# Layernorm with residual: x and residual loaded 16 rows at a time instead of 8, the stores moved ahead of the residual loads, and the last residual load split in 120 and 8 partitions

## The chip, the cores and the metric

The kernel runs on one core of a Trainium2 chip. The metric is device time in microseconds (us). The profiled span is about 1.3 us shorter than the time of the same execution. A transfer "lands" when the last increment of its semaphore comes; the trace of the kernel before shows 16 increments for each load of x or residual and each store, and does not name the DMA engines that they come from. The DMA share is the page's: the mean busy share of the core's 16 DMA engines.

In this text ACT is ScalarE, DVE is VectorE, POOL is GpSimd and SP is SyncE, which issues the loads of x and residual and all stores. "Row" is one row of 512 float32 (2 KB) in each of the 128 partitions; the problem has 128 such rows, and 8 of them are 2 MB.

## The reference

```python
def reference(x, residual, gamma, beta, eps):      # x, residual: [16, 1024, 512] float32
    z = x + residual
    mean = np.mean(z, axis=-1, keepdims=True)
    var = np.var(z, axis=-1, keepdims=True)
    return gamma * (z - mean) / np.sqrt(var + eps) + beta
```

So 67.1 MB are read and 33.6 MB written.

## The kernel before

Each engine has one part of the work. SP loads x into a ring of 64 rows and the residual into a ring of 32 rows, and stores the result out of the x ring. POOL adds 8 rows at a time. ACT takes 4 rows at a time: a pass for the mean, a pass for the sum of squares, and a small square root. DVE follows with two passes for each row, in place.

SP's loop decides the order of the transfers. All go through one queue: the page of the kernel before has 6336 of its 6341 packets in q1, and its 44 transfers landed in the order of their issue, each with its first increment after the last one of the transfer before. So an entry stands behind all that were issued before it:

```python
X_CHUNKS = [8] * 15 + [4, 4]
R_CHUNKS = [8] * 15 + [4, 4]
OUT_CHUNKS = [16] * 7 + [8, 4, 4]
Z_ROWS, R_ROWS, STORE_LAG = 64, 32, 40

    for c, (lo, n) in enumerate(loads_x):
        asked = lo + n
        while stored < asked - Z_ROWS:          # the x ring: wait until a block has been stored
            ...
            nc.sync.wait_ge(so[o], 16)
        move(part(zbuf, Z_ROWS, lo, n), dram(xf, lo, n), sx[c])
        while todo_r and ... <= asked:
            wait_rows(s_add, "add", rlo + rn - R_ROWS)      # the residual ring
            move(part(rbuf, R_ROWS, rlo, rn), dram(rf, rlo, rn), sr[rc])
        while todo_o and (... <= asked - STORE_LAG or asked == total):
            wait_rows(s_out, "out", olo + on)
            move(dram(of, olo, on), part(zbuf, Z_ROWS, olo, on), so[oc])
    ...
    for c, (lo, n) in enumerate(loads_x):       # POOL
        nc.gpsimd.wait_ge(sx[c], 16)
        for rc, (rlo, rn) in enumerate(loads_r):
            if lo <= rlo < lo + n:
                nc.gpsimd.wait_ge(sr[rc], 16)
                for a in range(rlo, rlo + rn, ADD):         # ADD = 8
                    nc.gpsimd.tensor_tensor(out=z, in0=z, in1=..., op=ALU.add).then_inc(s_add, an)
    # ... cut: ACT and DVE loops, 4 rows a group, two groups a turn
```

Of the kernel before, what the change touches and what calls it, by code (L numbers as in the profile page):

```python
# [10 lines left out]
ALU = mybir.AluOpType  # L11


X_CHUNKS = [8] * 15 + [4, 4]
R_CHUNKS = [8] * 15 + [4, 4]
OUT_CHUNKS = [16] * 7 + [8, 4, 4]

Z_ROWS = 64
R_ROWS = 32
STORE_LAG = 40  # L20


ADD = 8
# [11 lines left out]
def kernel(  # L35
# [9 lines left out]
    nc = tc.nc  # L45
    P = nc.NUM_PARTITIONS
    xf = x.flatten_outer_dims()
    rf = residual.flatten_outer_dims()
    of = out.flatten_outer_dims()
    N, D = xf.shape  # L50
    inv_d = 1.0 / float(D)
    total = N // P
# [5 lines left out]
    def spans(sizes):  # L58
        assert sum(sizes) == total
        return [(sum(sizes[:c]), n) for c, n in enumerate(sizes)]  # L60

    blocks = spans(OUT_CHUNKS)

    def dram(t, lo, n):

        b0, bn = next(b for b in blocks if b[0] <= lo and lo + n <= b[0] + b[1])
        v = t[P * b0 : P * (b0 + bn), :].rearrange("(p j) d -> p j d", p=P)
        return v[:, lo - b0 : lo - b0 + n, :].rearrange("p a b -> p (a b)")

    zbuf = nc.alloc_sbuf_tensor("zbuf", [P, Z_ROWS * D], FP32)  # L70
    rbuf = nc.alloc_sbuf_tensor("rbuf", [P, R_ROWS * D], FP32)
# [17 lines left out]
    def sem(name):  # L89
        s = nc.alloc_semaphore(name)  # L90
        sems.append(s)
        return s

    loads_x, loads_r, stores = spans(X_CHUNKS), spans(R_CHUNKS), blocks
    sx = [sem(f"sx{c}") for c in range(len(loads_x))]
    sr = [sem(f"sr{c}") for c in range(len(loads_r))]
# [7 lines left out]
    s_out = sem("out")  # L104
    so = [sem(f"so{c}") for c in range(len(stores))]
# [3 lines left out]
    def part(buf, size, lo, n):  # L109
        assert lo % size + n <= size  # L110
        return buf[:, (lo % size) * D : (lo % size + n) * D]
# [16 lines left out]
    todo_r, todo_o = list(enumerate(loads_r)), list(enumerate(stores))  # L128
# [3 lines left out]
    def wait_rows(s, key, rows):  # L132
        if rows > seen[key]:
            nc.sync.wait_ge(s, rows)
            seen[key] = rows

    def move(out, in_, s):
        i = nc.sync.dma_start(out=out, in_=in_).then_inc(s, 16)  # L138
        if len(first) < EARLY:
            first.append(i.ins)  # L140

    stored = 0
    for c, (lo, n) in enumerate(loads_x):
        asked = lo + n
        while stored < asked - Z_ROWS:
            o = next(i for i, b in enumerate(stores) if b[0] == stored)
            assert all(o != t[0] for t in todo_o)
            nc.sync.wait_ge(so[o], 16)
            stored += stores[o][1]
        move(part(zbuf, Z_ROWS, lo, n), dram(xf, lo, n), sx[c])  # L150
        while todo_r and todo_r[0][1][0] + todo_r[0][1][1] <= asked:
            rc, (rlo, rn) = todo_r.pop(0)
            wait_rows(s_add, "add", rlo + rn - R_ROWS)
            move(part(rbuf, R_ROWS, rlo, rn), dram(rf, rlo, rn), sr[rc])
        while todo_o and (
            todo_o[0][1][0] + todo_o[0][1][1] <= asked - STORE_LAG or asked == total
        ):
            oc, (olo, on) = todo_o.pop(0)
            wait_rows(s_out, "out", olo + on)
            move(dram(of, olo, on), part(zbuf, Z_ROWS, olo, on), so[oc])  # L160



    for o, (lo, n) in enumerate(stores[:-1]):
# [7 lines left out]
    for c, (lo, n) in enumerate(loads_x):  # L172
        nc.gpsimd.wait_ge(sx[c], 16)
        for rc, (rlo, rn) in enumerate(loads_r):
            if lo <= rlo < lo + n:
                assert rlo + rn <= lo + n
                nc.gpsimd.wait_ge(sr[rc], 16)
                for a in range(rlo, rlo + rn, ADD):
                    an = min(ADD, rlo + rn - a)
                    z = part(zbuf, Z_ROWS, a, an)  # L180
                    nc.gpsimd.tensor_tensor(  # L181
                        out=z, in0=z, in1=part(rbuf, R_ROWS, a, an), op=ALU.add
                    ).then_inc(s_add, an)
# [8 lines left out]
    with act.Fori(0, total // LAP) as lap:  # L192
        z0 = act.snap((lap * (LAP * D)) % (Z_ROWS * D))
        r0 = act.snap(lap * LAP)
        for j in range(SETS):
# [4 lines left out]
            for k in range(TURN):  # L200
                i = act.activation(  # L201
                    out=junk_m[k][:, :],
# [7 lines left out]
            for k in range(TURN):  # L210
                i = act.activation(  # L211
                    out=junk_s[k][:, :],
# [8 lines left out]
                out=std[j][:, :],  # L221
# [9 lines left out]
    with dve.Fori(0, total // LAP) as lap:  # L231
        z0 = dve.snap((lap * (LAP * D)) % (Z_ROWS * D))
        r0 = dve.snap(lap * LAP)
        for j in range(SETS):
# [3 lines left out]
            for k in range(TURN):  # L238
                dve.scalar_tensor_tensor(  # L239
                    out=zk[k],  # L240
# [9 lines left out]
            for k in range(TURN):  # L250
                i = dve.scalar_tensor_tensor(  # L251
                    out=zk[k],
# [53 lines left out]
```

## Time and profile before

| | before |
|---|---|
| time, median | 239.19 us (239.16 to 239.43, 4 runs) |
| profiled span | 237.9 us |
| ACT, DVE, POOL busy | 78%, 74%, 60% |
| DMA | 100.7 MB, mean 423 GB/s |

From the page of the kernel before, part 2, the span in 40 equal slices (5.9 us each); a digit is the busy share in tenths, and the last line is what the DMA engines moved:

```profile
ACT  2003999999999999999999999739996399999600
POOL 0098988989889407893078930889209892770000
DMA  8999999999999999999999999999999999999996
GB/s 309 441 433 421 433 433 433 419 427 441 421 438 419 438 427 424 468 441 386 427 433 435 441 413 433 430 449 430 413 430 419 457 441 383 455 435 430 421 417 287
```

DMA is at 9 from the second slice to the next to last. ACT has holes, in the second half too: there it waits for rows. The view by windows of the kernel before puts numbers to it. The columns are the stretch, its length, the busy time (and instructions) of PE, PEld, DVE, ACT and POOL, the clock, the DMA share and GB/s:

```profile
12.00:60.00 48.00, 0.00 (x0) 0.00 (x0) 30.77 (x51) 37.21 (x111) 43.84 (x5) 1.00 1.01 430
...
110.00:169.00 59.00, 0.00 (x0) 0.00 (x0) 49.08 (x81) 51.39 (x152) 35.46 (x4) 1.00 1.00 429
169.00:210.00 41.00, 0.00 (x0) 0.00 (x0) 32.88 (x55) 34.22 (x103) 23.75 (x4) 1.00 1.01 431
210.00:238.00 28.00, 0.00 (x0) 0.00 (x0) 17.92 (x30) 13.22 (x39) 3.02 (x1) 1.00 0.92 396
```

From 110 to 169 us, ACT is busy for 51.39 of 59 us, from 169 to 210 for 34.22 of 41, and DVE for less, while the DMA share is 1.00 and 1.01. The kernel is DMA-bound. The waits view of the kernel before says what ACT's holes wait for (total, times, longest):

```profile
ACT junk_m L201 <- POOL zbuf L181: 29.1, 4, 17.4
```

POOL in turn waits for residual loads, as POOL's timeline of the kernel before shows (start, duration, idle before, releaser). The lines are the adds of rows 96 to 103, 104 to 111 and 112 to 119:

```profile
159.40 8.84 POOL L181 TENSOR_TENSOR zbuf<-zbuf,rbuf 128x4096 f32<-128x4096 f32 x1 [0.90 <-DMA rbuf<-in_residual_dram]
179.00 8.86 POOL L181 TENSOR_TENSOR zbuf<-zbuf,rbuf 128x4096 f32<-128x4096 f32 x1 [10.75 <-DMA rbuf<-in_residual_dram]
188.77 8.85 POOL L181 TENSOR_TENSOR zbuf<-zbuf,rbuf 128x4096 f32<-128x4096 f32 x1 [0.91 <-DMA rbuf<-in_residual_dram]
```

The end of the kernel before, from its timeline: the last two stores are issued, the last ACT group ends with its square root, and DVE ends the last rows:

```profile
223.31 6.12 SPq L138 DMA_DIRECT2D out_dram<-zbuf  x2
223.46 0.30 ACT L220 ACTIVATE std<-ssq,eps_t 128x4 f32<-128x4 f32 x1
...
226.35 2.72 DVE L251 SCALAR_TENSOR_TENSOR zbuf<-zbuf,rstd,beta_p 128x512 f32 x4
```

The last result is ready at 229.1 us, but its store, only 1 MB, lands at 237.86 us (the trace's semaphore increments). The store before it landed at 235.35.

### The profile page before, as it was taken

The numbers are of one execution on the slowest core, as the hardware profiler recorded it, in microseconds if no ns is written. First come the engines' busy times: TensorE is split into PE (matmuls) and PEld (weight loads), VectorE is DVE, ScalarE is ACT, GpSimd is POOL, SyncE is SP. The second block draws the span as 40 slices with busy tenths as digits, with TensorE's granted clock in tenths as the row PEclk, the third lists the DMA queues.
The fourth block names the chain that finished last, engine by engine and source line by source line (L and its number), as shares of the span: only waits on it lengthen the run. The fifth ranks groups of instructions, "written<-read, shape, count | busy, mean of one in ns | idle before, by whom it ended". The sixth has DMA issues, their size and how long they took to land.

```text
span 237.9 us, 1484 instructions
## 1 busy us (share of the span) xinstructions
PE 3.7 (2%) x4; PEld 1.2 (0%) x4; DVE 177.2 (74%) x290; ACT 185.5 (78%) x545; POOL 142.2 (60%) x21
## 2 busy tenths in 40 slices
PE   0600000000000000000000000000000000000000
PEld 0100000000000000000000000000000000000000
DVE  0000498989898989898989898963989549898950
ACT  2003999999999999999999999739996399999600
POOL 0098988989889407893078930889209892770000
DMA  8999999999999999999999999999999999999996
GB/s 309 441 433 421 433 433 433 419 427 441 421 438 419 438 427 424 468 441 386 427 433 435 441 413 433 430 449 430 413 430 419 457 441 383 455 435 430 421 417 287
DMA packets 6341, 100.68 MB, mean 423 GB/s; under 512 B 706, under 2 KB 706, under 8 KB 708
## 3 DMA queue, kind: packets, MB, share of 16 engines
q1 hardware_dynamic: 6336, 100.67, 99.3%
q14 instruction: 1, 0.01, 0.0%
q10 hardware_dynamic: 4, 0.00, 0.0%
HBM read 67.11 MB, written 33.55 MB: 423 GB/s over the span
## 4 chain that ended last, share of the span: by engine, by line
DMA 49%; ACT 24%; POOL 11%; DVE 5%; issue 4%; SPq 1%; ACTq 1%; DVEq 0%; POOLq 0%
DMA rbuf<-in_residual_dram 36%; ACT junk_s L211 14%; DMA out_dram<-zbuf 13%; POOL zbuf L181 11%; ACT junk_m L201 10%; DVE zbuf L239 3%; DVE zbuf L251 3%; SPq L138 1%; ACTq L201 1%; DVEq L239 0%; ACT std L220 0%; DVE rstd L248 0%; ACTq L192 0%; ACTq L198 0%; DVEq L231 0%
## 5 line engine op out<-in xcount | busy, mean ns | idle before, releaser
L181 POOL TENSOR_TENSOR zbuf<-zbuf,rbuf 128x4096 f32<-128x4096 f32 (+1 forms) x17 | 142.0, 8353 | 70.6 <-DMA rbuf<-in_residual_dram 70.6
L239 DVE SCALAR_TENSOR_TENSOR zbuf<-zbuf,nm,gamma_p 128x512 f32 x128 | 87.1, 742 | 48.7 <-ACT junk_s L211 48.7
L201 ACT ACTIVATE junk_m<-zbuf 128x512 f32 x128 | 74.8, 585 | 31.5 <-POOL zbuf L181 29.1
L211 ACT ACTIVATE junk_s<-zbuf,nm 128x512 f32 x128 | 88.9, 695 | 1.0
L251 DVE SCALAR_TENSOR_TENSOR zbuf<-zbuf,rstd,beta_p 128x512 f32 x128 | 87.1, 743 | 1.1
L211 ACT ACTIVATION_READ_ACCUMULATOR junk_s<-zbuf,nm 128x1 f32 x128 | 23.9, 187 | 0.0
L201 ACT ACTIVATION_READ_ACCUMULATOR junk_m<-zbuf 128x1 f32 x128 | 23.9, 186 | 0.0
L220 ACT ACTIVATE std<-ssq,eps_t 128x4 f32<-128x4 f32 x32 | 9.5, 297 | 3.0
L248 DVE RECIPROCAL rstd<-std 128x4 f32<-128x4 f32 x32 | 5.4, 170 | 0.0
L189 ACT ACT_TABLE_LOAD x1 | 1.3, 1283 | 2.7 <-PEq L56 2.7
L123 PE MATMUL gamma_p<-gb_row,ones 1*128 1x512 f32 x2 | 2.0, 1118 | 7.2 <-DMA gb_row<-in_gamma_dram 7.2
L123 PE MATMUL beta_p<-gb_row,ones 1*128 1x512 f32 x2 | 1.9, 1052 | 0.0
L118 DVE MEMSET ones<- 1x128 f32 x1 | 0.2, 165 | 2.0 <-PEq L56 2.0
L123 PEld LDWEIGHTS beta_p<-gb_row,ones 1*128 1x128 f32 x2 | 0.7, 328 | 1.0 <-issue 0.5
L123 PEld LDWEIGHTS gamma_p<-gb_row,ones 1*128 1x128 f32 x2 | 0.5, 308 | 7.2 <-issue 7.2
L287 POOL MEMSET const-float32-0.0<- 128x1 f32 x1 | 0.1, 99 | 0.2 <-issue 0.2
L287 POOL MEMSET const-bfloat16-1.0<- 128x1 bf16 x1 | 0.1, 102 | 0.0
L287 POOL MEMSET const-uint8-127<- 128x1 uint8 x1 | 0.1, 102 | 0.0
L287 POOL MEMSET const-float32-1.0<- 128x1 f32 x1 | 0.1, 99 | 0.0
L119 DVE MEMSET eps_t<- 128x1 f32 x1 | 0.1, 59 | 0.0
## 6 DMA issues: line engine op xcount, KB each, us to landing
zbuf<-in_x_dram SPq DMA_DIRECT2D x15, 2048.0 KB, 32.9
rbuf<-in_residual_dram SPq DMA_DIRECT2D x15, 2048.0 KB, 30.1
out_dram<-zbuf SPq DMA_DIRECT2D x7, 4096.0 KB, 28.5
zbuf<-in_x_dram SPq DMA_DIRECT2D x2, 1024.0 KB, 32.5
rbuf<-in_residual_dram SPq DMA_DIRECT2D x2, 1024.0 KB, 34.5
out_dram<-zbuf SPq DMA_DIRECT2D x1, 2048.0 KB, 15.7
out_dram<-zbuf SPq DMA_DIRECT2D x2, 1024.0 KB, 10.4
gb_row<-in_gamma_dram ACTq DMA_DIRECT2D x1, 2.0 KB
```

Of the source, the lines that this page charges most:

```text
L118: nc.vector.memset(ones[:, :], 1.0).then_inc(s_const, 1)
L123: nc.tensor.matmul(dest[:, :], ones[:, :], gb_row[:, k * D : (k + 1) * D], start=True, stop=True).then_inc(s_pe, 1)
L138: i = nc.sync.dma_start(out=out, in_=in_).then_inc(s, 16)
L181: nc.gpsimd.tensor_tensor(out=z, in0=z, in1=part(rbuf, R_ROWS, a, an), op=ALU.add).then_inc(s_add, an)
L189: act.preload_act_table_set("sqrt_and_others")
L201: i = act.activation(out=junk_m[k][:, :], in_=zk[k], func=ACT.Identity, scale=-inv_d, accum_out=nm[j][:, k : k + 1],)
L211: i = act.activation(out=junk_s[k][:, :], in_=zk[k], func=ACT.Square, bias=nm[j][:, k : k + 1], accum_out=ssq[j][:, k : k + 1],)
L220: act.activation(out=std[j][:, :], in_=ssq[j][:, :], func=ACT.Sqrt, bias=eps_t[:, 0:1], scale=inv_d,).then_inc(s_std, TURN)
L239: dve.scalar_tensor_tensor(out=zk[k], in0=zk[k], scalar=nm[j][:, k : k + 1], in1=gamma_p[:, :], op0=ALU.add, op1=ALU.mult,)
L248: dve.reciprocal(out=rstd[j][:, :], in_=std[j][:, :]).then_inc(s_dve, TURN)
L251: i = dve.scalar_tensor_tensor(out=zk[k], in0=zk[k], scalar=rstd[j][:, k : k + 1], in1=beta_p[:, :], op0=ALU.mult, op1=ALU.add,)
L287: nc = _bacc.Bacc("TRN2", target_bir_lowering=False, num_devices=1)
```

## The change

The intent is fewer and larger transfers: loads of 32 KB for each partition instead of 16 KB, as the stores already were. With these loads each store is put ahead of the residual load of its step, so that the residual load stands behind the store in the queue while the next x load still waits for that store to land. The split cuts the last residual load in 120 and 8 partitions; the prediction reads it as relief for an engine that ends late.

```diff
-X_CHUNKS = [8] * 15 + [4, 4]
-R_CHUNKS = [8] * 15 + [4, 4]
-OUT_CHUNKS = [16] * 7 + [8, 4, 4]
+BLOCK = 16
+TAIL = [8, 4, 4]
+X_CHUNKS = [BLOCK] * 7 + TAIL
+R_CHUNKS = [BLOCK] * 7 + TAIL
+OUT_CHUNKS = [BLOCK] * 7 + TAIL
-STORE_LAG = 40
+STORE_LAG = 48
+SPLIT = 120
+    def store_to(rows):
+        while todo_o and todo_o[0][1][0] + todo_o[0][1][1] <= rows:
+            ... wait_rows(s_out, "out", olo + on); move(dram(of, olo, on), part(zbuf, ...), so[oc])
         move(part(zbuf, Z_ROWS, lo, n), dram(xf, lo, n), sx[c])
+        if n == BLOCK:
+            store_to(asked - STORE_LAG)
         while todo_r and ... <= asked:
             wait_rows(s_add, "add", rlo + rn - R_ROWS)
-            move(part(rbuf, R_ROWS, rlo, rn), dram(rf, rlo, rn), sr[rc])
-        while todo_o and (... <= asked - STORE_LAG or asked == total): ...
+            cuts = [0, P] if rlo + rn < total else [0, SPLIT, P]
+            for p0, p1 in zip(cuts, cuts[1:]):
+                move(part(rbuf, ...)[p0:p1, :], dram(rf, ...)[p0:p1, :], sr[rc])
+    store_to(total)
-                nc.gpsimd.wait_ge(sr[rc], 16)
+                nc.gpsimd.wait_ge(sr[rc], 16 if rlo + rn < total else 32)
```

More of the change, by code (lines that the diff above doesn't have):

```diff
@@ L140, in move @@
             first.append(i.ins)
+    def store_to(rows):
+        while todo_o and todo_o[0][1][0] + todo_o[0][1][1] <= rows:
+            oc, (olo, on) = todo_o.pop(0)
+            wait_rows(s_out, "out", olo + on)
+            move(dram(of, olo, on), part(zbuf, Z_ROWS, olo, on), so[oc])
     stored = 0
@@ L153 @@
             wait_rows(s_add, "add", rlo + rn - R_ROWS)
-            move(part(rbuf, R_ROWS, rlo, rn), dram(rf, rlo, rn), sr[rc])
-        while todo_o and (
-            todo_o[0][1][0] + todo_o[0][1][1] <= asked - STORE_LAG or asked == total
-        ):
-            oc, (olo, on) = todo_o.pop(0)
-            wait_rows(s_out, "out", olo + on)
-            move(dram(of, olo, on), part(zbuf, Z_ROWS, olo, on), so[oc])
+            cuts = [0, P] if rlo + rn < total else [0, SPLIT, P]
+            for p0, p1 in zip(cuts, cuts[1:]):
+                move(
+                    part(rbuf, R_ROWS, rlo, rn)[p0:p1, :],
+                    dram(rf, rlo, rn)[p0:p1, :],
+                    sr[rc],
+                )
+    store_to(total)
     for o, (lo, n) in enumerate(stores[:-1]):
```

## The prediction

> **What bounds the kernel now.** The DMA engines. By windows of the profile their busy share is 1.00 to 1.01 from 12 to 210 us, moving 429 to 431 GB/s, and 100.7 MB passes in a span of 237.9 us (the measured time is 1.3 us more). ScalarE (ACT) is next, 78%: one group of 4 rows takes 5.85 us in the chain of waits, and two groups end 11.98 us apart where it never waits, so 128 rows cost about 191 us. It sits idle 29.1 us in all behind the add on GpSimd (POOL; waits view). The end is balanced: the timeline has the last ACT group end at 223.4, the output ready at 229.1, its 1 MB store issued then and landed only at 237.86 behind earlier stores. So the ACT chain has about 4 us of slack.
>
> **What the change does, costed.**
> - Loads of 32 KB per partition for 16 KB. Per engine, two 16 KB packets take 2 x 612 ns and a 32 KB packet 1213 ns (packet times, landing distances). 112 packets and 14 completions per engine go: about 1.2 us of DMA time saved.
> - The split: [...] The last store's landings show one engine 1.2 us behind; if it is that one, up to 0.7 us is saved, but only if the queue is full to the end.
> - Later start: the first add waits for 8 MB, not 4 MB: estimated residual landing 21.8 instead of 12.2 us, so ACT starts at about 31 instead of 21.4 us. It had idle time later, so this alone may cost nothing.
> - Coarser arrival and later residuals: the store of a block now stands ahead of the residual load of the same step. Rows 96 to 111 of the residual land at about 177.6 us (as many bytes ahead of it as of rows 104 to 111 now, landing at 178.8, less 1.2). Now, ACT has done rows 96 to 103 by then; after the change it has 8 groups left, not 6.
>
> **Critical path after.** A recurrence with these durations gives 236.8 us for before (without the late engine's 1.1). For after: residual 96 to 111 landed 177.6; first 8 rows added 8.9 us later, 186.6; 8 ACT groups, 47.5 us, end at about 234; DVE tail 5.7, output at 239.8; a 1 MB store on an empty queue: 2.5 us plus about 2 us of start and landing (the first load shows 7.3 for 4.9 of transfer). The queue, full until about 216 us, runs dry before each of the last four stores. Span about 244.2, so the DMA saving and the split's gain are both lost, because the tail is no longer DMA-bound.
>
> **Prediction.** 245.4 us, range 243.6 to 247.2. Faster by over 2%: 0.01; within 2%: 0.19; slower by over 2%: 0.80.
>
> **What would show it.** Right: first POOL add at about 22 us; ACT idle 3 times before POOL adds after 126 us, by about 1.5, 5 and 5 us; add of rows 96 to 103 beginning near 178; last ACT group ending near 234; DMA share below 1 after 216; no gap in DMA before 210. Wrong: ACT ending before 229, or DMA busy to the end.
>
> **What would make it wrong.** Larger packets gaining more than 1%; a bubble in the queue where a load waits for a store (margin about 7 us); POOL adding faster back to back; the last small store taking less than 4 us unqueued.

The lateness is measured: in the kernel before, the last store's last increment came at 237.86 us, the next at 237.15 and the median one at 236.54; the 0.7 us agree with the first of these differences. 177.6 for the late residual, 8.9 for the add, 47.5 for eight groups of ACT, 5.7 for DVE and some 4.5 for the last store make a span of 244.2, and with the 1.3 outside the span about 245.4 us.

## The result, and the profile after

The changed kernel takes 245.56 us in the median (245.49 to 245.74, 4 runs), against 239.19 us: slower, with a ratio of 1.0262 (95% interval 1.0248 to 1.0277). Its profiled span is 244.2 us.

From the page of the changed kernel, part 2 (slices of 6.1 us):

```profile
ACT  2000089999999999999978999199973999999940
POOL 0003997997998019970399506992089999900000
DMA  8999999999999999999999999999999999999874
GB/s 344 430 429 429 429 429 429 429 429 435 429 424 429 429 429 429 429 429 429 429 435 435 435 429 435 440 429 429 413 427 411 391 318 435 429 413 429 376 306 173
```

At the end ACT is now full and the DMA engines are not, the reverse of before. One slice of the last quarter, with 318 GB/s, falls out of line; more on that below. By windows, the changed kernel:

```profile
110.00:169.00 59.00, 0.00 (x0) 0.00 (x0) 48.17 (x80) 49.96 (x148) 35.36 (x4) 1.00 1.00 432
169.00:210.00 41.00, 0.00 (x0) 0.00 (x0) 32.92 (x55) 34.26 (x103) 31.80 (x5) 1.00 1.01 405
210.00:244.00 34.00, 0.00 (x0) 0.00 (x0) 28.20 (x46) 23.94 (x71) 3.66 (x1) 1.00 0.82 351
```

After 210 us, ACT has 23.94 us of work left, where it had 13.22 before: the difference is 10.7 us, or close to two groups of 4 rows. From the waits view of the changed kernel, ACT's waiting for adds:

```profile
ACT junk_m L212 <- POOL zbuf L192: 40.3, 4, 27.1
```

This total has grown by 11.2 us, and 9.7 us of that belong to the longest wait (27.1 against 17.4), the one at the start. By this line alone one would blame the late start. A total doesn't say which wait matters, though, and e7 below tests that reading.

POOL's timeline of the changed kernel shows where it comes from. Its first add starts later, and from there on the adds come in pairs (or more), the first of each stretch released by a residual load:

```profile
22.06 17.59 POOL L192 TENSOR_TENSOR zbuf<-zbuf,rbuf 128x4096 f32<-128x4096 f32 x2 [21.63 <-DMA rbuf<-in_residual_dram]
...
148.87 17.67 POOL L192 TENSOR_TENSOR zbuf<-zbuf,rbuf 128x4096 f32<-128x4096 f32 x2 [11.41 <-DMA rbuf<-in_residual_dram]
178.19 35.46 POOL L192 TENSOR_TENSOR zbuf<-zbuf,rbuf 128x4096 f32<-128x4096 f32 x5 [11.65 <-DMA rbuf<-in_residual_dram]
```

The second line is rows 80 to 95, and the third begins with rows 96 to 103. Before, they were added from 159.40 us on; now from 178.19. Their residual came in a load of its own ahead of the store of rows 48 to 63; now it is half of a larger load behind that store. The chain of waits of the changed kernel (start, duration, what) leads from there to the end through ACT; "x8" is one group's squares, and four more groups stand where lines are left out in the middle:

```profile
140.08 37.96 DMA rbuf<-in_residual_dram
...
178.19 8.87 POOL zbuf L192
...
189.87 2.94 ACT junk_s L222 x8
...
195.72 2.94 ACT junk_s L222 x8
...
225.75 2.94 ACT junk_s L222 x8
...
231.60 2.94 ACT junk_s L222 x8
```

Eight groups follow the last wait; in the kernel before it was six, for rows 104 to 127. Its last wait of ACT for an add, from ACT's timeline of the kernel before:

```profile
188.08 0.60 ACT L201 ACTIVATE junk_m<-zbuf 128x512 f32 x1 [5.63 <-POOL zbuf L181]
```

The end of the changed kernel, from its timeline:

```profile
228.31 12.29 SPq L141 DMA_DIRECT2D out_dram<-zbuf  x3
...
234.63 0.30 ACT L231 ACTIVATE std<-ssq,eps_t 128x4 f32<-128x4 f32 x1
...
237.52 2.72 DVE L262 SCALAR_TENSOR_TENSOR zbuf<-zbuf,rstd,beta_p 128x512 f32 x4
```

The last result is ready at 240.25 us, 11.2 us later than before. Its store lands at 244.12, after 3.9 us instead of 8.8, because nothing stands ahead of it. So 4.9 of the 11.2 us were slack before (8.8 less 3.9), and the rest, 6.3 us, is the loss in the span (244.2 against 237.9).

### The profile page after: what moved, and what is told of

It is laid out like the page before. It is cut to its first block, busy times and chain, and to the rows that moved or that the text cites. A ratio compares the mean times of both kernels' runs of the same rounds, so it can differ in the third digit from the quotient of the medians. Undisturbed runs are those within 1.5% of the kernel's fastest.

```text
span 244.2 us, 1464 instructions
## 1 busy us (share of the span) xinstructions
PE 4.1 (2%) x4; PEld 1.0 (0%) x4; DVE 177.2 (73%) x290; ACT 185.5 (76%) x545; POOL 141.7 (58%) x21
## 4 chain that ended last, share of the span: by engine, by line
DMA 47%; ACT 33%; POOL 7%; issue 5%; DVE 4%; ACTq 1%; SPq 1%; DVEq 0%; POOLq 0%
DMA rbuf<-in_residual_dram 24%; DMA out_dram<-zbuf 22%; ACT junk_s L222 19%; ACT junk_m L212 14%; POOL zbuf L192 7%; DVE zbuf L250 2%; DVE zbuf L262 2%; ACTq L212 1%; SPq L141 1%; ACT std L231 0%; ACTq L203 0%; DVEq L250 0%; ACTq L209 0%; ACTq L230 0%; DVE rstd L259 0%
```

## The experiments

Theory A: the end is set by ACT's groups after the late landing of the residual of rows 96 to 111, and so by the size of the loads. The rivals: the order of stores and residual loads costs in itself; ACT's later start costs; the queue still sets the end; and for the split, that it helps by freeing a late engine. All medians are beside the kernel before on the same chip: 239.11 us for e1 to e4, 239.39 for e6 to e9, 239.16 for e5, e10 and e11, which ran last.

| run | what | time, us | ratio to before (95%) |
|---|---|---|---|
| e1_small_loads | changed kernel, 8-row loads, no split | 239.29 | 1.0006 (0.9989 to 1.0023) |
| e2_split_only | before, last residual load in 120 + 8 partitions | 242.25 | 1.0132 (1.0115 to 1.0148) |
| e3_no_split | changed kernel, no split | 245.77 | 1.0285 (1.0268 to 1.0302) |
| e4_residual_small | e3 with residual loads of 8 rows | 241.24 | 1.0091 (1.0074 to 1.0108) |
| e5_store_last | e3 with stores after the residual loads | 251.58 | 1.0520 (1.0502 to 1.0537) |
| e6_small_late | 16-row loads early, 8-row loads late, no split | 239.03 | 0.9988 (0.9975 to 1.0002) |
| e7_small_first | e3 with the first block in two loads | 245.90 | 1.0273 (1.0258 to 1.0289) |
| e8_split_rows | before, last residual load in 2 + 2 rows | 239.46 | 1.0005 (0.9989 to 1.0020) |
| e9_split_halves | before, last residual load in 64 + 64 partitions | 242.29 | 1.0127 (1.0108 to 1.0146) |
| e10_scalar_light | e3 with a lighter ACT pass. Its output is wrong, which doesn't matter for the time. | 241.59 | 1.0104 (1.0086 to 1.0121) |
| e11_before_scalar_light | before with the same. Its output is wrong, which doesn't matter for the time. | 239.50 | 1.0010 (0.9994 to 1.0027) |

### Size or order: e1_small_loads

```diff
 (of the changed kernel)
-X_CHUNKS = [BLOCK] * 7 + TAIL
-R_CHUNKS = [BLOCK] * 7 + TAIL
+X_CHUNKS = [8] * 15 + [4, 4]
+R_CHUNKS = [8] * 15 + [4, 4]
-        if n == BLOCK:
-            store_to(asked - STORE_LAG)
+        store_to(asked - STORE_LAG)
-            cuts = [0, P] if rlo + rn < total else [0, SPLIT, P]
+            cuts = [0, P]
 # ... cut: POOL waits for 16 again, not 32, for the last residual load
```

> The changed kernel's store order and store lag, but loads of 8 rows as before and no split. Theory A (the loss comes from the size: rows 96 to 103 of the residual wait for rows 104 to 111 and for the store ahead of them): time back at that of the kernel before, 239.2 us (238.4 to 240.0), last ScalarE group ending near 224, DMA busy to the end. Rival B (the loss comes from putting each store ahead of the residual load): 242 us or more, last ScalarE group ending after 229.

It took 239.29 us, the same as before (239.11). The last ACT group of e1_small_loads, from ACT's timeline:

```profile
223.43 0.30 ACT L230 ACTIVATE std<-ssq,eps_t 128x4 f32<-128x4 f32 x1
```

That is within 0.03 us of the kernel before, although the order and the lag are those of the changed kernel. Rival B falls: with 8-row loads the order alone costs nothing. There, the residual of rows 96 to 103 isn't tied to what stands behind it.

### Which loads: e4_residual_small

```diff
 (of e3_no_split)
-R_CHUNKS = [BLOCK] * 7 + TAIL
+R_CHUNKS = [8] * 15 + [4, 4]
```

> The changed kernel with x still in loads of 16 rows and the residual in loads of 8, no split. Theory A (what counts is when the first 8 rows of the residual of rows 96 to 111 land, 4.9 us earlier here): last ScalarE group ends near 229.7, time 241.3 us (240.4 to 242.2), between the two kernels. Rival B (the order of stores alone counts): 245.5 us. Rival C (only the size of the residual loads counts): 239.2 us.

It took 241.24 us, with the last ACT group's square root at 230.18 us against 234.69 in e3. Smaller residual loads alone give back 4.5 us of the loss; smaller x loads as well, which is e1, the last 2.0 us. Both rivals fall.

### The order's use: e5_store_last

```diff
 (of e3_no_split)
-        if n == BLOCK:
-            store_to(asked - STORE_LAG)
         while todo_r and ... <= asked:
             ...
+        if n == BLOCK:
+            store_to(asked - STORE_LAG)
```

> The changed kernel without the split, its stores issued after the residual load of the same step, the order of the kernel before. Theory A (with 16-row loads each x load that waits for a store finds nothing behind that store in the queue): the DMA engines run dry about 2 us at each of 4 steps (near 90, 121, 152 and 184 us), the last ScalarE group ends earlier, near 231, and yet the time is 246.5 us (245.6 to 247.5). Rival B (the store ahead of the residual is in itself what costs, so undoing it gains): 242 us or less.

The direction was right and the size was not: 251.58 us, 5 us more than expected. The expected end of ACT was missed too: its last square root came at 234.81 us, as in e3 (234.69), and not near 231. The queue sets the end again: the last store is issued at 240.45 us and lands only at 249.84. The windows of e5 show the holes:

```profile
75.00:90.00 15.00, 0.00 (x0) 0.00 (x0) 14.07 (x24) 14.52 (x44) 13.07 (x3) 1.00 0.92 387
90.00:95.00 5.00, 0.00 (x0) 0.00 (x0) 4.74 (x9) 4.68 (x14) 5.00 (x1) 1.00 0.86 315
```

In SP's timeline of e5 the x load that waits for the first store is issued only when that store has landed:

```profile
60.40 0.35 SPq L141 DMA_DIRECT2D out_dram<-zbuf  x1
90.31 0.33 SPq L141 DMA_DIRECT2D zbuf<-in_x_dram  x1
```

A 4 MB transfer lands 9.7 us after the one ahead of it where the queue is full. At each of the first three restarts the x load landed 12.2 us after the store, and the residual load behind it another 10.6 us later: 3.4 us lost each time (12.2 + 10.6 less twice 9.7), not about 2 as in the estimate, which had left out slow packets: 95 of the 32 KB packets took over 1.5 times the median of 1213 ns in e5, against 19 in e3. At each of these restarts they are 10 to 13 of the first packets, and again 15 or 16 packets of the residual load, some 19 us later; why the latter are slow isn't known.

So to undo the change's order is no remedy: with 16-row loads and this lag the order is worth 5.8 us (251.58 against 245.77). It isn't shown that the store ahead of the residual load costs nothing with such loads. In e5 the residual of rows 96 to 111 landed at 178.24 us, and at 178.09 in e3: the 9.7 us of the store that was no longer ahead of it went to the three restarts (3 times 3.4 us). A shorter lag, which could keep the queue full with the stores last, was not run.

### The late start: e7_small_first

```diff
 (of e3_no_split)
-X_CHUNKS = [BLOCK] * 7 + TAIL
-R_CHUNKS = [BLOCK] * 7 + TAIL
+X_CHUNKS = [8, 8] + [BLOCK] * 6 + TAIL
+R_CHUNKS = X_CHUNKS
```

> The changed kernel without the split, its first block loaded in two parts of 8 rows, so that GpSimd and ScalarE start 9 us earlier. Theory A (ScalarE's late start is made up, because it later waits for loads anyway): first add near 12.4 us, and the same time as without this edit, 245.7 us (245.2 to 246.2). Rival B (the late start is the loss): 240 us or less.

The first add started at 12.42 us, as in the kernel before, and the time was 245.90 us, no better than e3's 245.77 (from another call; the ratios to before are 1.0273 and 1.0285). ACT's late start costs nothing, because ACT waits for the last loads later anyway.

### ACT's chain itself: e10_scalar_light and e11_before_scalar_light

```diff
 (of e3_no_split and of the kernel before; the result is wrong on purpose)
-                    out=junk_m[k][:, :],
-                    in_=zk[k],
+                    out=junk_m[k][:, : D // 2],
+                    in_=zbuf[:, bass.ds(z0 + (j * TURN + k) * D, D // 2)],
```

> Wrong result on purpose: the changed kernel without the split, with ScalarE's mean pass over 256 of the 512 columns, so each group of 4 rows is shorter by an estimated 0.6 to 1.1 us. Theory A (eight ScalarE groups after the last wait set the end): last group ends 5 to 8 us earlier, at 226 to 230, and the time falls by 5 us or more, to 240.5 us or less, until the DMA queue binds again near 239. Rival B (the end is set by landing times or by the queue): within 1 us of 245.7.

> Wrong result on purpose: the kernel before with the same lighter mean pass. Theory A (it is DMA-bound to its end, with ScalarE in slack): the time stays at 239.2 us (238.6 to 239.8). Rival B (ScalarE's chain sets its end too): 236 us or less.

The kernel before didn't gain (239.50 us): ACT isn't what bounds it. The changed kernel without the split fell from 245.77 to 241.59 us: its end does depend on the compute chain. That is 4.2 us rather than the 5 or more that were expected. The last ACT group ended 6.7 us earlier (square root at 228.00 us, against 234.69): the lighter mean pass took 0.36 to 0.39 us in e10's timeline from 200 to 210 us, the full one 0.585 in the mean (page of the changed kernel), which makes some 0.8 us for a group of 4 rows, within the range estimated. But DVE became the next limit. From DVE's timeline of e10, the last two groups stand back to back:

```profile
225.24 2.72 DVE L250 SCALAR_TENSOR_TENSOR zbuf<-zbuf,nm,gamma_p 128x512 f32 x4
227.87 0.17 DVE L259 RECIPROCAL rstd<-std 128x4 f32<-128x4 f32 x1
228.08 2.72 DVE L262 SCALAR_TENSOR_TENSOR zbuf<-zbuf,rstd,beta_p 128x512 f32 x4
230.72 2.72 DVE L250 SCALAR_TENSOR_TENSOR zbuf<-zbuf,nm,gamma_p 128x512 f32 x4
```

A group costs DVE 5.48 us from start to start, only half a microsecond less than it cost ACT (11.98 us for two), so little could be gained before DVE took over.

### The split: e2_split_only, e3_no_split, e8_split_rows, e9_split_halves

The odd slice of the changed kernel's page is where the split load passes. Most of its packets of 8 KB took 540 to 630 ns there (median 605) and not 309. Hence these runs.

```diff
 (e2, of the kernel before; e9 has 64 in place of 120)
-            move(part(rbuf, R_ROWS, rlo, rn), dram(rf, rlo, rn), sr[rc])
+            cuts = [0, P] if rlo + rn < total else [0, 120, P]
+            for p0, p1 in zip(cuts, cuts[1:]):
+                move(part(rbuf, ...)[p0:p1, :], dram(rf, ...)[p0:p1, :], sr[rc])
-                nc.gpsimd.wait_ge(sr[rc], 16)
+                nc.gpsimd.wait_ge(sr[rc], 16 if rlo + rn < total else 32)
 (e3, of the changed kernel)
-            cuts = [0, P] if rlo + rn < total else [0, SPLIT, P]
+            cuts = [0, P]
 # ... cut: POOL's wait goes back to 16 with it
 (e8, of the kernel before: the same two loads, cut along the rows)
+            cuts = [0, rn] if rlo + rn < total else [0, rn // 2, rn]
 # ... cut: the moves take these rows of all partitions; POOL waits for 32 at the last load
```

> The kernel before with only its last residual load split in 120 and 8 partitions. Theory A (read from the changed kernel's trace, where 8 KB packets of that load took 500 to 640 ns and not 309): the last residual load takes 2.2 us longer, and since the kernel before is DMA-bound to its end, the time goes to 241.3 us (240.4 to 242.2). Rival B (the recorded reading: the split relieves the late engine): 238.5 us, up to 0.7 less than before.

> The changed kernel without the split. Theory A (the end is set by ScalarE, the split's 2.2 us of DMA time lie in slack): same time as the changed kernel, 245.5 us (245.1 to 245.9), with the last residual landing about 2 us earlier and the DMA engines idle about 1.5 us more before the store of rows 96 to 111. Rival B (the end is still set by the queue): 243.3 us.

> The kernel before with its last residual load split in two along the rows (2 and 2 rows, all 128 partitions each), a control for the split by partitions. Theory A [...]: packets of 4 KB at about 160 ns, the same time as before, 239.3 us (239.0 to 239.8). Rival B (two loads for one are slow in themselves): 241 us or more.

> The kernel before with its last residual load split in partitions 0 to 63 and 64 to 127. Theory A [...]: 8 KB packets of this load at about 600 ns as in the 120 and 8 split, load 2.5 us longer, time 241.5 us (240.9 to 242.5), and no engine ahead of the others after it. Rival B [...]: packets stay at 309 ns, time 239.2 us.

What is left of theory A is that the cut by partitions costs and a cut along the rows doesn't; e9's rival was that the cost needs the odd part of 8.

In the kernel before, which is DMA-bound to its end, the split alone costs 3.1 us (242.25 us, just above the expected range, and no gain as the recorded reading had it). The same 5 us by windows, first in the kernel before:

```profile
204.00:209.00 5.00, 0.00 (x0) 0.00 (x0) 4.37 (x8) 4.88 (x16) 4.59 (x2) 1.00 1.05 446
```

and in e2_split_only:

```profile
204.00:209.00 5.00, 0.00 (x0) 0.00 (x0) 4.37 (x8) 4.88 (x16) 3.87 (x1) 1.00 1.07 262
```

The engines are as busy and move 262 instead of 446 GB/s. The last residual load, at the median of its increments, lands 4.8 us after the load ahead of it, against 2.47. Afterwards one of the 16 increments of a store comes 4.6 us ahead of the median one (in the changed kernel too, in the store behind the split load: 205.33 against 209.94 us), so something was relieved; but another still comes 1.3 us behind the next slowest in the last store (240.85 against 239.59), so what was relieved wasn't what was late.

In the changed kernel the split costs nothing: without it the time is 245.77 us, against 245.56 (not the same rounds; the ratios to before, 1.0285 and 1.0262, overlap in their intervals). The queue there had slack to lose. The changed kernel's windows line for 221 to 228 us:

```profile
221.00:228.00 7.00, 0.00 (x0) 0.00 (x0) 6.74 (x12) 6.68 (x22) 0.00 (x0) 1.00 1.01 435
```

and that of e3_no_split:

```profile
221.00:228.00 7.00, 0.00 (x0) 0.00 (x0) 6.74 (x12) 6.68 (x22) 0.00 (x0) 1.00 0.75 323
```

Without the split the DMA engines idle a quarter of this stretch, waiting for ACT and DVE; with it they are still working off the delay.

Cutting the load in two isn't what costs: e8, two loads along the rows, took 239.46 us, with 4 KB packets at 160 ns. Cutting by partitions is: e9, two halves of 64 partitions, took 242.29 us, its 8 KB packets at about 610 ns, and none of the increments got ahead by more than 1 us. So an odd part of 8 partitions isn't needed for the cost. The packets of the 120 and 8 partitions (606 ns at the median in e2) and of the two halves take about the same time, twice the 309 ns of the kernel before; why the parts are slow, no run here shows.

### A version between the two: e6_small_late

```diff
 (of the changed kernel, without the split)
-X_CHUNKS = [BLOCK] * 7 + TAIL
-R_CHUNKS = [BLOCK] * 7 + TAIL
+X_CHUNKS = [BLOCK] * 5 + [8] * 5 + [4, 4]
+R_CHUNKS = X_CHUNKS
-        if n == BLOCK:
-            store_to(asked - STORE_LAG)
+        store_to(asked - STORE_LAG)
```

> The changed kernel with 16-row loads for the first five blocks (80 rows) only, 8-row loads for the next five, then 4 and 4; no split. Theory A (small loads are needed only where ScalarE catches up with the loads, at the end; large ones save DMA time everywhere else): DMA-bound to the end again, last ScalarE group near 224, time 238.4 us (237.8 to 239.1), 0.3% under the kernel before. Rival B (large loads early cost something too, by the later start of ScalarE): 240 us or more.

It took 239.03 us against 239.39, a ratio of 0.9988 whose interval (0.9975 to 1.0002) just includes 1, in five rounds. Its first add started at 22.24 us and its last ACT group still ended with the square root at 223.99: the large loads do no harm early. It is 6.7 us under e3, so only the late loads matter to the loss. That it beats the kernel before isn't shown: the gain of 0.3% that was expected came out at 0.1%.

## Why the prediction was right

The range holds, and so does the mechanism. That the span came out at 244.2 us to the tenth is in part luck: the late residual landed 0.4 us later than predicted, and the last store was some 0.6 us quicker.

**What bounds the kernel before** was right. Its time didn't move when ACT's work became lighter (e11: 239.50 us against 239.16), and rose when the last residual load became slower (e2: 242.25 against 239.11).

**The late residual and eight groups of ACT** were right, to within a microsecond: residual of rows 96 to 111 landed at 178.04 us (177.6 predicted), last ACT group ended at 234.54 (234), result ready at 240.25 (239.8), span 244.2 (244.2). ACT's waits before the last three late adds were about 2.3, 5.4 and 5.6 us (1.5, 5 and 5 predicted). e1, e4 and e10 confirm that this chain sets the time.

**The part of the order** lacked its condition. The prediction names, beside coarser arrival, that the store now stands ahead of the residual load. e1 has this order and loses nothing (239.29 us); e5 undoes it and loses more (251.58), because the queue then runs dry. It is the 16-row load that ties rows 96 to 103 to a place in the queue behind rows 104 to 111 of x and behind the store. How much the store's place costs by itself with 16-row loads, no run separates.

**The later start** costs nothing, as the prediction supposed (e7).

**The DMA time saved by larger packets** was mis-sized: 1.2 us were predicted. With the same 72 MiB moved by then in both kernels, its own bytes included, the residual of rows 96 to 111 landed 0.8 us earlier at the last increment (178.04 against 178.84) and 0.3 us at the median one (177.82 against 178.10). In e6 the whole time fell by 0.4 us, within noise. What ate the rest stays open. It isn't the length of packets in the stream: the typical 32 KB packet took 1213 ns, as estimated.

**The split** was wrong in direction. "Up to 0.7 us is saved" was the step; its load took 2.3 us longer instead (4.8 against 2.47), 3.1 us of the time where the queue binds (e2). The prediction took the packets' duration over from loads of 128 partitions, 309 ns in the kernel before, and the relief of the late engine was its estimate. That it didn't spoil the sum is owed to the slack at the end of the changed kernel, which the prediction had seen. In consequence "the queue runs dry before each of the last four stores" came true in full only without the split; with it, the store of rows 96 to 111 still found a queue to stand in (DMA share 1.01 from 221 to 228 us, against 0.75).

**The last store on an empty queue** took 3.9 us, against some 4.5 in the estimate.

## What to carry to other kernels

This DMA-bound kernel had a compute chain beside it with 4 to 5 us of slack at the end, and its timeline and landings showed that beforehand. Before loads are made larger, count how many compute groups stand behind the last late load. Here there were eight groups of 5.85 us and no longer six, as rows 96 to 103 waited for the rows that they were now lumped with and for the store ahead of them, and were added from 178.19 us, not from 159.40. Large loads early and small ones late kept that chain short (e6: last square root at 223.99 us, against 234.69 in e3), but the larger packets themselves brought almost nothing here: 0.3 to 0.8 us of 178, and no gain in the whole time that five rounds could show (e6). If a transfer must be cut, the cut along the rows cost nothing here (e8: 239.46 us against 239.39), and those by partitions cost 3.1 us (e2) and 2.9 us (e9). And keep something in the queue behind a store that a load waits for: without it each of the first three restarts lost 3.4 us with 4 MB transfers (e5), 2.5 of it on the x load after the pause and 0.9 on the residual load behind that.
